# Products of 512 columns for the weight tiles outside U, with the bank's halves added by ScalarE and VectorE

## The chip, the cores and the metric

The kernel runs on one core of a Trainium2 chip. The metric is the device time of the program in microseconds (us), the median of several runs. Engines go by their names in the profile: PE is TensorE, DVE is VectorE, ACT is ScalarE, POOL is GpSimd, SP is SyncE, which issues the loads.

## The reference

256 tokens of width 1024 go through two blocks in float32. Cut to what matters here:

```python
def first_block(x, ...):
    z = rmsnorm(x, norm_gain) @ w_in
    a_in, a_gate, q, k, v, b_gp, g_logits = split(z)
    y_a = (multiscale_pool(a_in) * silu(a_gate)) @ w_proj_a
    y_b = (dilated_attention(q, k, v) * silu(b_gp)) @ w_proj_b
    gates = sigmoid(g_logits + b_gate)
    x = x + (gates[0] * y_a + gates[1] * y_b) @ w_out
    return rmsnorm(x, final_gain)

def second_block(x, ...):
    x = x + short_conv_mixer(rmsnorm(x))       # (gate_b * conv3(gate_c * h)) @ w_out
    x = x + peer(rmsnorm(x), layer 0)
    x = x + windowed_gqa(rmsnorm(x))           # q: 16 heads, k and v: 4 heads
    x = x + peer(rmsnorm(x), layer 1)
    return rmsnorm(x)

def peer(t):
    sc = (t @ w_q) against two sets of 128 subkeys, 8 heads
    idx, g = top 16 of the 16 x 16 best pairs, softmax
    h = t . u_tab[idx]
    return sum over idx of g * gelu(h) * v_tab[idx]
```

The kernel computes `peer` densely: all 16384 rows of `u_tab` meet all tokens (stage U), and `v_tab` likewise (stage V).

## The kernel before

The normed tokens stand transposed, 1024 channels as eight groups `k` of 128 partitions, with 256 tokens in a row. To keep float32 accuracy a value is held as two parts of the faster format `fp32r`: a high part, rounded, and a low part, the rest. Of two such numbers the kernel forms three products: high by high, high by low, low by high. The tokens' parts are `xh` and `xl`.

A weight tile is 128x1024: eight square pieces, one for each `k`, that give 128 outputs. `dense_t` (line 140) handles one: `fetch` has SP load it into `raw`; `split` (line 106) has ScalarE cast the high part `hi` (line 122) and VectorE, for some tiles POOL, subtract to get the low part `lo` (line 123); then `products` (line 133) makes 24 products of 256 columns (lines 136 to 138) that add up in the first half of a PSUM bank:

```python
        for i, ((ah, al), (bh, bl)) in enumerate(pairs):
            PE.matmul(out=ps, lhsT=ah, rhs=bh, start=first and i == 0, stop=False)
            PE.matmul(out=ps, lhsT=ah, rhs=bl, start=False, stop=False)
            PE.matmul(out=ps, lhsT=al, rhs=bh, start=False, stop=last and i == n - 1)
```

Weights come first in the product's names (`lhsT`), tokens second. `hi` and `lo` have three buffers each (`HL`), so the cast of tile t+3 waits for the last product of tile t. The banks of these tiles come from the pool `p_mm`, which has two; transposes (`p_tr`) have two, scores and accumulators (`p_acc`) four, which makes eight in all. The caller reads the bank and so sets it free.

The callers, in the program's order, and the number of tiles that the change touches:

- `qk` (line 622), 24 tiles of queries and keys of the first attention. The first six follow on each other; among the rest stand scores, transposes and values. Consumers are ScalarE's copies and, for group 0, `stacked` (line 149), two of ScalarE and two of VectorE.
- `rest` (line 508), 12 tiles: pooling input, `gate_a`, `gate_b`. The consumer is one ScalarE copy (lines 511 and 514); a silu follows for each gate (lines 523 and 524).
- `gate` (line 544), 16 tiles: a sigmoid on ScalarE (line 547). Four come first, then two before each `merge`, which has a weight tile of its own that is not changed.
- `streamed` in `conv_mixer` (line 722), 20 tiles in groups of three: gate `gb`, `gc` and `h`. ScalarE copies `gb` and `gc` (line 727); `h` stays in its bank until VectorE's `pr` (line 746) has multiplied it by `gc`. The sums of the short convolution (lines 750 and 752), `z` (line 756) and the parts `o` (lines 402 and 403) follow. ScalarE and VectorE also split a tile of the output weights for each group (`kept`).
- `query` of `peer` (line 955), 12 tiles in each of two layers: a ScalarE copy (line 957), then two products with the subkeys and VectorE's lists (from line 974).
- `query` of `gqa_mixer` (line 796), 8 tiles: `stacked` into `q_t` (lines 153 and 155), among scores (line 811), transposes and weighted sums.

Stage U (line 1171) calls `dense_t` for 256 tiles, and 360 tiles make up the 2880 products of each line. A scheduler orders the instructions of each engine at build time from the program's order; the split is issued with a priority 200 steps ahead (`AHEAD`), so that casts and subtractions come before work that stands earlier in the program. Each engine then runs its list strictly in that order, and waits where an instruction's input, or the room for its output, is not there.

Of the kernel before, what the change touches and what calls it, by code (L numbers as in the profile page):

```python
# [11 lines left out]
F32R = mybir.dt.float32r  # L12
# [3 lines left out]
AF = mybir.ActivationFunctionType  # L16
# [34 lines left out]
def two_blocks(ctx: ExitStack, tc: tile.TileContext, io, out):  # L51
# [26 lines left out]
    x = const.tile([P, 2, D], F32, name="x")  # L78
    sums = [const.tile([P, 4], F32, name=f"ss{a}") for a in range(2)]
    squares = const.tile([P, 512], F32, name="squares")  # L80
    xh = const.tile([P, 8, T], F32R, name="xh")
    xl = const.tile([P, 8, T], F32R, name="xl")
    iota_f = const.tile([P, P], BF16, name="iota_f")
    G.iota(iota_f, pattern=[[1, P]], base=0, channel_multiplier=0,
           allow_small_or_imprecise_dtypes=True)
# [20 lines left out]
    def split(raw, pool_share=0, into=None):  # L106
        with tc.high_priority(offset=AHEAD):
            return split_now(raw, pool_share, into)
# [31 lines left out]
    def dense_t(src, acts, pool_share=0):  # L140

        ah, al = acts
        hi, lo = split(fetch(src), pool_share)
        ps = bank(p_mm, "mm")[:, :T]
        products(ps, [((hi[:, k * P:(k + 1) * P], lo[:, k * P:(k + 1) * P]), (ah[:, k], al[:, k]))
                      for k in range(8)], True, True)
        return ps

    def stacked(ps, dst):

# [271 lines left out]
    def first_block(nxt):  # L422
        acts = xh, xl
        with ExitStack() as es:
# [81 lines left out]
                V.tensor_tensor(out=pooled[g], in0=pooled[g], in1=u[:, g, 8:8 + T], op=OP.subtract)  # L506

            def rest(n):
                ps = dense_t(io["w_rest"][n], acts)
                if n < 8:  # L510
                    S.copy(out=as_ordered(gate_a[:, n % 4] if n >= 4 else u[:, n, 8:8 + T]),
                           in_=ordered(ps))
                else:
                    S.copy(out=gate_b[:, n % 4], in_=ps)
                if 4 <= n < 8:
                    window(n - 4)
# [27 lines left out]
            def gate(n, i):  # L544
                c = 8 * i + n
                gt = w2.tile([P, T], F32, tag=f"gt{i}", name=f"gt{i}", bufs=3)
                S.activation(out=gt, in_=dense_t(io["w_rest"][12 + c], acts), func=AF.Sigmoid,
                             bias=b_gate[:, c:c + 1])
                gates[n, i] = gt

# [44 lines left out]
    def attention(acts, es1, at1, v_n, att, rest, loads):  # L595
# [25 lines left out]

        def qk(hp, g):
            n = g * 4 + hp
            ps = dense_t(io["w_qk"][n], acts, 2)
            if g:
                S.activation(out=q_t[hp][:, g - 1], in_=ps, func=AF.Copy, scale=0.125)
            else:
                stacked(ps, q_2[hp])
            ps = dense_t(io["w_qk"][12 + n], acts, 2)
            if g:  # L630
                S.copy(out=k_t[hp][:, g - 1], in_=ps)
                return
            for e, mine, _ in HALVES:
                S.copy(out=k_2[hp][mine, e], in_=ps[mine])
            for e, mine, _ in HALVES:
                V.tensor_tensor(out=k_l[hp][mine], in0=ps[mine], in1=k_2[hp][mine, e].bitcast(F32),  # L636
                                op=OP.subtract)
            for e, mine, other in HALVES:
                G.tensor_copy(out=k_2[hp][other, e], in_=k_2[hp][mine, e])
# [70 lines left out]
    def conv_mixer(entered, nxt):  # L710
        acts, nat = (xh, xl), entered.nat
        with ExitStack() as es:
# [7 lines left out]
            keep = keeper(cv, io["conv_w_out"])  # L720

            def streamed():
                return dense_t(io["conv_w_in"][next(tiles)], acts)

            def copied(tag):
                t = w2.tile([P, T], F32, tag=tag, name=tag)
# [37 lines left out]
    def gqa_mixer(entered, nxt):  # L764
        acts, nat = (xh, xl), entered.nat
        with ExitStack() as es:
# [27 lines left out]
            zl = b1.tile([P, 8, T], F32R, name="zl")  # L794

            def query(n):
                stacked(dense_t(io["attn_w_q"][n], acts, 3), q_t[:, 2 * n:2 * n + 2])

            def place(i):

# [127 lines left out]
    def peer(l, entered, nxt):  # L928
        acts, nat = (xh, xl), entered.nat
        with ExitStack() as es:  # L930
            with ExitStack() as es1:
# [19 lines left out]
                def query(n):  # L951
                    if n < 4:
                        q[n] = first[:, n]
                        return
                    ps = dense_t(io["peer_w_q"][l, n - 4], acts, 2)
                    q[n] = X[1][:, n].rearrange("p g t -> p (g t)")
                    S.copy(out=q[n], in_=ps)

# [419 lines left out]
```

## Time and profile before

| what | value |
|---|---|
| median of 3 runs | 2127.23 us (2122.63 to 2131.82) |
| profiled execution, its own time | 2128.48 us |
| its span | 2126.7 us |
| mean granted clock of PE | 0.992 of full speed |
| PE busy | 2089.0 us, 98% |
| PEld (weight loads, beside the products) busy | 1899.0 us, 89% |
| DVE, ACT, POOL busy | 1519.2, 1095.3, 216.4 us |
| DMA | 373.94 MB, mean 176 GB/s |

The page comes from the profiled execution. Its span runs from the first to the last recorded instruction. A busy time is a share of the whole; what a wait costs is read in the stage where it stands.

### The profile page before, as it was taken

To read this page: it belongs to the slowest core of one execution; us is meant where nothing else is said; L and a number is where in the kernel's file an instruction comes from. 1 tells how busy PE (TensorE), PEld (TensorE's weight loads), DVE (VectorE), ACT (ScalarE), POOL (GpSimd) and SP (SyncE) were. 2 spreads that over 40 slices of the span, in tenths; PEclk is the share of its full clock that TensorE was granted. 3 is DMA by queue.
4 is the path that set the end of the run, shared out by engine and by line. 5 is a ranking of instruction groups with operands and counts; after the bars stand their busy time and mean duration, and the time that the engine had idled before them with its cause. 6 is when DMAs were issued, how large, how long until landed. Compare 5 with 4: busy or idle time off the path is not lost. (4 is left out here: it accounts for less than half of the span.)

```text
span 2126.7 us, 37692 instructions
## 1 busy us (share of the span) xinstructions
PE 2089.0 (98%) x14288; PEld 1899.0 (89%) x14288; DVE 1519.2 (71%) x3101; ACT 1095.3 (52%) x1971; POOL 216.4 (10%) x119
## 2 busy tenths in 40 slices
PE   8999999999999999999999999999999999999998
PEld 7899989899999999888888777999999998888886
DVE  4456778699778887655656685998778885656565
ACT  4556645345555444555555574455554445555554
POOL 3220011162000000000000241540000000000000
PEclk9999999999999999999999999999999999999999
DMA  6645737255655555666666571566555556666664
GB/s 235 219 128 158 244 114 247 89 171 177 180 163 165 159 160 168 192 193 190 194 191 199 181 230 50 165 185 182 161 164 163 160 165 195 195 189 192 194 189 138
DMA packets 104437, 373.94 MB, mean 176 GB/s; under 512 B 12096, under 2 KB 14144, under 8 KB 103744
## 3 DMA queue, kind: packets, MB, share of 16 engines
q1 hardware_dynamic: 103968, 371.01, 56.1%
q8 instruction: 112, 1.84, 0.3%
q14 instruction: 69, 0.57, 0.1%
q10 hardware_dynamic: 288, 0.52, 0.1%
HBM read 370.44 MB, written 1.05 MB: 175 GB/s over the span
## 5 line engine op out<-in xcount | busy, mean ns | idle before, releaser
L123 DVE TENSOR_TENSOR lo<-raw,hi 128x1024 fp32r<-128x1024 f32 x532 | 650.6, 1223 | 260.2 <-ACT hi L122 256.9
L136 PE MATMUL mm<-xh,hi 128*128 128x256 f32 x2880 | 830.4, 288 | 0.4 <-DVE k_l L636 0.4
L138 PE MATMUL mm<-xh,lo 128*128 128x256 f32 x2880 | 814.3, 283 | 0.4 <-DVE lo L123 0.4
L137 PE MATMUL mm<-xl,hi 128*128 128x256 f32 x2880 | 814.1, 283 | 0.0
L122 ACT CAST hi<-raw 128x1024 fp32r<-128x1024 f32 x600 | 630.1, 1050 | 337.4 <-PE mm L137 192.9
L136 PEld LDWEIGHTS mm<-xh,hi 128*128 128x128 f32 x2880 | 551.5, 191 | 2.3 <-issue 1.3
L137 PEld LDWEIGHTS mm<-xl,hi 128*128 128x128 f32 x2880 | 551.8, 192 | 0.3
L138 PEld LDWEIGHTS mm<-xh,lo 128*128 128x128 f32 x2880 | 551.2, 191 | 0.8 <-DVE lo L123 0.8
L1204 PE MATMUL acc<-hi,al 128*128 128x512 f32 x976 | 304.1, 393 | 0.0
L1204 PE MATMUL acc<-lo,ah 128*128 128x512 f32 x976 | 302.4, 391 | 0.0
L1204 PE MATMUL acc<-hi,ah 128*128 128x512 f32 x976 | 301.5, 390 | 0.0
L1204 PEld LDWEIGHTS acc<-hi,ah 128*128 128x128 f32 x976 | 183.1, 188 | 41.8
L1204 PEld LDWEIGHTS acc<-hi,al 128*128 128x128 f32 x976 | 183.3, 188 | 39.7
L1204 PEld LDWEIGHTS acc<-lo,ah 128*128 128x128 f32 x976 | 183.3, 188 | 38.7
L1193 ACT CAST ah<-xa 128x256 fp32r<-128x256 f32 x200 | 81.2, 407 | 241.5 <-PE acc L1204 241.5
L123 POOL TENSOR_TENSOR lo<-raw,hi 128x1024 fp32r<-128x1024 f32 x70 | 171.6, 2452 | 267.5 <-ACT hi L122 256.0
L1194 DVE TENSOR_TENSOR al<-xa,ah 128x256 fp32r<-128x256 f32 x200 | 85.0, 426 | 99.0 <-PE acc L1204 99.0
L1109 DVE TENSOR_TENSOR o<-iota_k,ij 128x1024 f16<-128x1024 f16 x128 | 88.2, 689 | 48.5 <-PE G L1123 48.2
L298 POOL TENSOR_TENSOR enl<-raw,enh 128x1024 fp32r<-128x1024 f32 x5 | 12.4, 2478 | 867.3 <-ACT enh L297 867.3
L1133 ACT COPY xa<-G 128x240 f32<-128x240 f32 (+22 forms) x92 | 24.1, 262 | 148.2 <-DVE xa L1130 148.2
L1116 DVE TENSOR_TENSOR wi<-o,gt 128x512 f16<-128x512 f16 x256 | 96.5, 418 | 1.2
L1123 PE MATMUL G<-wi,o 128*128 128x128 f16 x1024 | 79.8, 220 | 0.0
(461 smaller groups left out, 2029.6 us busy)
## 6 DMA issues: line engine op xcount, KB each, us to landing
raw<-in_peer_u_dram SPq DMA_DIRECT2D x256, 512.0 KB, 3.6
raw<-in_peer_v_dram SPq DMA_DIRECT2D x256, 512.0 KB, 4.1
raw<-in_peer_w_q_dram SPq DMA_DIRECT2D x24, 512.0 KB, 3.7
raw<-in_conv_w_in_dram SPq DMA_DIRECT2D x20, 512.0 KB, 4.4
raw<-in_w_rest_dram SPq DMA_DIRECT2D x18, 512.0 KB, 3.7
raw<-in_w_qk_dram SPq DMA_DIRECT2D x16, 512.0 KB, 4.3
more<-in_w_rest_dram SPq DMA_DIRECT2D x10, 512.0 KB, 3.7
raw<-in_w_v_dram SPq DMA_DIRECT2D x8, 512.0 KB, 4.3
```

Source lines behind the costliest of these rows:

```text
L122: S.copy(out=hi, in_=raw)
L123: low = (G if on_pool else V).tensor_tensor(out=lo, in0=raw, in1=hi.bitcast(F32), op=OP.subtract)
L136: PE.matmul(out=ps, lhsT=ah, rhs=bh, start=first and i == 0, stop=False)
L137: PE.matmul(out=ps, lhsT=ah, rhs=bl, start=False, stop=False)
L138: PE.matmul(out=ps, lhsT=al, rhs=bh, start=False, stop=last and i == n - 1)
L1109: V.tensor_tensor(out=o.rearrange("p n (b c) -> p n b c", c=4), in0=iota_k.rearrange("p (b c) -> p b c", c=4).unsqueeze(1).to_broadcast(fo ...
L1116: V.tensor_tensor(out=wi[i].rearrange("p n (b c) -> p n b c", c=4), in0=o[:, 0:4].rearrange("p n (b c) -> p n b c", c=4), in1=gt[i][:, s]. ...
L1123: PE.matmul(out=ps[:, :, t], lhsT=o[:, 4 + t], rhs=wi[i][:, t], start=i == 0, stop=i == 1)
L1133: S.copy(out=dst[:, old:], in_=ps[:, i0 + old:i0 + n])
L1193: S.copy(out=act[0], in_=src)
L1194: V.tensor_tensor(out=act[1], in0=src, in1=act[0].bitcast(F32), op=OP.subtract)
L1204: PE.matmul(out=acc[a][half], lhsT=p[:, s], rhs=r[:, half * 512:(half + 1) * 512], start=i == 0 and w == 0, stop=i == P - 1 and w == 2)
```

## The change

The tokens' two parts become the halves of one tile `xx`, side by side for each `k`. A new function `dense_w` takes the place of `dense_t` in the six callers above; U keeps `dense_t`. For each `k` it makes one product of `hi` with 512 columns (`xh` and `xl`) into the whole bank, and one of `lo` with the 256 columns of `xh` into the first half: 16 products in place of 24. The second half of the bank then holds high by low. ScalarE copies it into one of the two halves of `squares`, and VectorE adds that to the first half, in the bank. Callers read the first half as before.

```diff
-    xh = const.tile([P, 8, T], F32R, name="xh")
-    xl = const.tile([P, 8, T], F32R, name="xl")
+    xx = const.tile([P, 8, 2, T], F32R, name="xx")
+    xh, xl = xx[:, :, 0], xx[:, :, 1]
...
+    def dense_w(src, pool_share=0):
+        hi, lo = split(fetch(src), pool_share)
+        ps = bank(p_mm, "mm")
+        for k in range(8):
+            s = slice(k * P, (k + 1) * P)
+            PE.matmul(out=ps, lhsT=hi[:, s], rhs=xx[:, k].rearrange("p w t -> p (w t)"),
+                      start=k == 0, stop=False)
+            PE.matmul(out=ps[:, :T], lhsT=lo[:, s], rhs=xh[:, k], start=False, stop=k == 7)
+        other = squares[:, count[0] % 2 * T:count[0] % 2 * T + T]
+        S.copy(out=other, in_=ps[:, T:])
+        V.tensor_tensor(out=ps[:, :T], in0=other, in1=ps[:, :T], op=OP.add)
+        return ps[:, :T]
...
-                ps = dense_t(io["w_rest"][n], acts)
+                ps = dense_w(io["w_rest"][n])
...
-                S.activation(out=gt, in_=dense_t(io["w_rest"][12 + c], acts), func=AF.Sigmoid,
+                S.activation(out=gt, in_=dense_w(io["w_rest"][12 + c]), func=AF.Sigmoid,
...
-            ps = dense_t(io["w_qk"][n], acts, 2)
+            ps = dense_w(io["w_qk"][n], 2)
...
-            ps = dense_t(io["w_qk"][12 + n], acts, 2)
+            ps = dense_w(io["w_qk"][12 + n], 2)
...
-                return dense_t(io["conv_w_in"][next(tiles)], acts)
+                return dense_w(io["conv_w_in"][next(tiles)])
...
-                stacked(dense_t(io["attn_w_q"][n], acts, 3), q_t[:, 2 * n:2 * n + 2])
+                stacked(dense_w(io["attn_w_q"][n], 3), q_t[:, 2 * n:2 * n + 2])
...
-                    ps = dense_t(io["peer_w_q"][l, n - 4], acts, 2)
+                    ps = dense_w(io["peer_w_q"][l, n - 4], 2)
```

The scheduler builds a new order from this. Three places show it. In these rows a name is a tile with its number, and the part behind the arrow is what is read; `mm` is a weight tile's bank. Numbers differ from one kernel to the other. The change's lines stand one lower in the helpers (123 for 122, 124 for 123), 16 lower in the callers (743 for 727, 762 for 746, 563 for 547); the new copy is line 161, the addition line 162.

ScalarE in the middle of the convolution, before:

```order
L122 CAST hi_3917<-raw_3915 128x1024
L727 COPY gb_3797<-mm_3804 128x256
L402 CAST o4h_3787<-z_3785 128x256
L122 CAST hi_3950<-raw_3948 128x1024
L727 COPY gc_3830<-mm_3837 128x256
L402 CAST kept4h_4027<-raw_4025 128x1024
L122 CAST hi_3982<-raw_3980 128x1024
L122 CAST hi_4034<-raw_4032 128x1024
```

The same place with the change (`mm_3326` is a gb tile, `mm_3353` the gc tile after it, `mm_3379` the h tile, which takes the bank of `mm_3326`; `hi_3448` takes the buffer of `mm_3353`'s high part):

```order
L123 CAST hi_3421<-raw_3419 128x1024
L161 COPY squares_81<-mm_3326 128x256
L418 CAST kept3h_3513<-raw_3511 128x1024
L123 CAST hi_3448<-raw_3446 128x1024
L418 CAST o3h_3309<-z_3307 128x256
L743 COPY gb_3319<-mm_3326 128x256
L161 COPY squares_81<-mm_3353 128x256
L743 COPY gc_3346<-mm_3353 128x256
L123 CAST hi_3474<-raw_3472 128x1024
L161 COPY squares_81<-mm_3379 128x256
L123 CAST hi_3520<-raw_3518 128x1024
```

Before, the copy of gb follows the cast that waits for the end of gb's own tile. With the change the copy of gb, two rows behind `hi_3448`, comes after a cast that waits for the end of the gc tile.

ScalarE at the first gate of the first block, before (`mm_2018` is the last `rest` tile, `mm_2058` the first gate):

```order
L122 CAST hi_2152<-raw_2150 128x1024
L514 COPY gate_b_282<-mm_2018 128x256
L524 ACTIVATE gate_b_282<-gate_b_282 128x1024
L122 CAST hi_2185<-more_2183 128x1024
L547 ACT_TABLE_LOAD
L547 ACTIVATE gt0_2051<-mm_2058,b_gate_286 128x256
```

With the change (`mm_1841` is the first gate; `hi_2009` takes the buffer of the second gate's high part):

```order
L123 CAST hi_1950<-more_1948 128x1024
L540 ACTIVATE gate_b_281<-gate_b_281 128x1024
L161 COPY squares_81<-mm_1841 128x256
L418 CAST yb0h_1900<-y_1898 128x256
L123 CAST hi_2009<-raw_2007 128x1024
L563 ACT_TABLE_LOAD
L563 ACTIVATE gt0_1834<-mm_1841,b_gate_285 128x256
```

The first gate's sigmoid followed one cast, and it now follows the second gate's cast, `hi_2009`, as well.

VectorE in the convolution, before:

```order
L123 TENSOR_TENSOR lo_3834<-raw_3831,hi_3833 128x1024
L403 TENSOR_TENSOR kept3l_3911<-raw_3908,kept3h_3910 128x1024
L746 TENSOR_TENSOR pr_3777<-mm_3752,gc_3713 128x4x4x16
L750 TENSOR_SCALAR y_3781<-pr_3777,taps_3338 128x256
L123 TENSOR_TENSOR lo_3866<-raw_3863,hi_3865 128x1024
```

With the change:

```order
L162 TENSOR_TENSOR mm_3353<-squares_81,mm_3353 128x256
L124 TENSOR_TENSOR lo_3475<-raw_3472,hi_3474 128x1024
L162 TENSOR_TENSOR mm_3379<-squares_81,mm_3379 128x256
L762 TENSOR_TENSOR pr_3398<-mm_3379,gc_3346 128x4x4x16
L766 TENSOR_SCALAR y_3402<-pr_3398,taps_3025 128x256
```

Between the low part of a later tile and the product `pr` there now stands the addition in the h tile's bank.

## Rows read from the trace of the kernel before

**Rows 1.** The page's part 1: engine, busy us (share of the span), instructions.

```profile
PE 2089.0 (98%) x14288; PEld 1899.0 (89%) x14288; DVE 1519.2 (71%) x3101; ACT 1095.3 (52%) x1971; POOL 216.4 (10%) x119
```

**Rows 2.** The page's part 5: group | busy, mean ns | idle before.

```profile
L136 PE MATMUL mm<-xh,hi 128*128 128x256 f32 x2880 | 830.4, 288 | 0.4 <-DVE k_l L636 0.4
```

**Rows 3.** Windows: us; busy of PE, PEld, DVE, ACT, POOL; PEclk, DMA, GB/s.

```profile
305.00:365.00 60.00, 60.00 (x488) 59.37 (x487) 50.85 (x78) 35.85 (x50) 2.41 (x1) 1.00 0.68 220
405.00:450.00 45.00, 44.92 (x380) 44.71 (x379) 41.75 (x240) 19.64 (x29) 21.59 (x9) 1.00 0.53 159
1240.00:1250.00 10.00, 6.96 (x32) 4.33 (x31) 8.38 (x16) 7.35 (x18) 6.33 (x4) 0.70 0.56 181
```

**Rows 4.** Timeline of ACT, convolution: start, us, what [idle before <-releaser].

```profile
329.66 1.05 ACT L122 CAST hi<-raw 128x1024 fp32r<-128x1024 f32 x1 [1.78 <-PE mm L137]
...
330.61 0.37 ACT L727 COPY gb<-mm 128x256 f32<-128x256 f32 x1
...
331.41 0.41 ACT L402 CAST o3h<-z 128x256 fp32r<-128x256 f32 x1 [0.44 <-DVE pr L745]
...
338.30 1.05 ACT L122 CAST hi<-raw 128x1024 fp32r<-128x1024 f32 x1 [1.78 <-PE mm L137]
```

**Rows 5.** Timeline of PE in the expert stage V.

```profile
1100.02 0.62 PE L1204 MATMUL acc<-lo,ah 128*128 128x512 f32 x2
...
1102.76 0.62 PE L1204 MATMUL acc<-lo,ah 128*128 128x512 f32 x2
```

**Rows 6.** Groups by line: two VectorE operations that read a bank.

```profile
L561 DVE TENSOR_TENSOR y<-pj,gt 128x256 f32<-128x256 f32 x16 | 6.5, 419 | 1.4 <-PE pj L138 1.4
...
L329 DVE TENSOR_TENSOR xl<-tr,xh 128x512 fp32r<-128x512 f32 x20 | 13.3, 688 | 18.0 <-ACT xh L328 17.9
```

**Rows 7.** Timeline of DVE in the convolution.

```profile
328.60 1.22 DVE L123 TENSOR_TENSOR lo<-raw,hi 128x1024 fp32r<-128x1024 f32 x1
...
329.74 1.00 DVE L752 SCALAR_TENSOR_TENSOR y<-pr,taps,y 128x256 f32<-128x256 f32 x2
...
336.36 0.60 DVE L746 TENSOR_TENSOR pr<-mm,gc 128x256 f32<-128x256 f32 x1
```

**Rows 8.** Waits of PE: line <- releaser: us in total, times, longest.

```profile
PE mm L136 <- DVE k_l L636: 0.4, 1, 0.4
...
PE acc L181 <- ACT o7h L402: 2.9, 1, 2.9
...
PE tr L413 <- DVE s L827: 4.9, 3, 3.0
```

**Rows 9.** Timeline of ACT from the last `rest` tiles to the first gate.

```profile
180.53 1.28 ACT L523 ACT_TABLE_LOAD   x1
...
181.82 1.06 ACT L523 ACTIVATE gate_a<-gate_a 128x1024 f32<-128x1024 f32 x1
...
196.47 1.28 ACT L547 ACT_TABLE_LOAD   x1
...
197.77 0.47 ACT L547 ACTIVATE gt<-mm,b_gate 128x256 f32<-128x256 f32 x1
```

**Rows 10.** Timeline of DVE, first expert query (MAX8 rows).

```profile
407.38 0.30 DVE L974 MAX8 xb<-sc 128x8 f32<-128x128 f32 x1 [10.07 <-PE sc L969]
...
422.89 0.30 DVE L974 MAX8 xb<-sc 128x8 f32<-128x128 f32 x1
```

**Rows 11.** Timeline of ACT in the first expert query.

```profile
409.09 1.05 ACT L122 CAST hi<-raw 128x1024 fp32r<-128x1024 f32 x1 [2.29 <-POOL lo L123]
...
422.37 1.05 ACT L122 CAST hi<-raw 128x1024 fp32r<-128x1024 f32 x1 [2.05 <-issue]
```

**Rows 12.** Timeline of ACT in window attention.

```profile
1226.17 1.05 ACT L122 CAST hi<-raw 128x1024 fp32r<-128x1024 f32 x1 [0.93 <-PE mm L137]
```

**Rows 13.** Timeline of DVE in window attention.

```profile
1227.92 0.87 DVE L155 SCALAR_TENSOR_TENSOR q_t<-mm,q_t 64x256 fp32r<-64x256 f32 x2 [0.91 <-ACT q_t L153]
```

**Rows 14.** Timeline of PE in window attention.

```profile
1237.73 0.60 PE L413 MATMUL tr<-ident,s 128*128 128x128 f32 x4
```

## The prediction

> **What bounds the kernel now.** I read the busy times first: TensorE is busy for 98% of the span, VectorE for 71%, ScalarE for 52% [rows 1]. Such a kernel ends earlier only where TensorE gets less to do, and later wherever TensorE is made to wait. Then the groups by line: the products of the weight tiles are 2880 on each of three lines, and the first of these lines has waited 0.4 us in all [rows 2]. So the 104 tiles that the change touches run without gaps now, and each new wait is paid in full. Then the stages: in a stretch of the convolution TensorE is busy for 60.00 of 60 us and VectorE for 50.85; in the expert query VectorE is busy for 41.75 of 45 [rows 3]. There VectorE has least to spare.
>
> **The products.** In the convolution every third tile has a cast that starts as the tile before ends, and these casts lie 8.64 us apart (329.66 and 338.30) [rows 4]: three tiles of 24 products, 0.1200 us each. Products of 512 columns stand in the expert stage V; the starts show twelve in 2.74 us, 0.2283 each [rows 5]. A tile costs 24 x 0.1200 = 2.880 us now, and 8 x (0.2283 + 0.1200) = 2.786 with the change: 0.094 less, and 9.7 us less for 104 tiles. That is the whole gain. The bounds: if the new pairs keep none of it, 0; if products cost their columns at 2.4 GHz and nothing else (6144 columns, 2.56 us), 0.32 per tile, 33 us. I take 9.7, since both intervals are rows.
>
> A rule of the Trainium skill speaks against this gain: "TensorE: Matmul & The Clock Gate", section "Back-to-back issue gap", gives an isolated product N/2.4 + 2.5 ns, so 109 and 216 ns here. By it a merged pair saves just 2.5 ns, an estimated 2 us for the 832 products that go, and the sum below would come out 8 us higher. The rows differ (120.0 and 228.3 ns, so a fixed part of some 13), and they decide. The section's sustained 131 ns for 512 columns is contradicted by the 228.3 likewise.
>
> **The added work.** Each tile gets a ScalarE copy of 128x256 (0.37 us, as at 330.61 [rows 4]) and a VectorE addition within the bank, which the trace does not show. The nearest rows are a product of bank and memory of the same size, 0.419, and a 128x512 subtraction that reads a bank, 0.688 [rows 6]. I take 0.42, as the size is the same; bounds 0.42 and 0.69. What costs is less the busy time than the place in the order.
>
> The pool has two banks. Before, tile t's bank is free after one consumer; now after copy, addition and consumer. The copy stands on ScalarE behind the cast of tile t+3's weights (1.05; the next starts 0.95 after it [rows 4]), since that cast takes the buffers that tile t held. The addition stands on VectorE behind the low part of those weights (1.22; the next starts 1.14 after it [rows 7]). And as the pieces of order show, ScalarE's consumers now stand behind the *next* tile's cast, which waits for the next tile's end: there the bank comes free after the tile that wanted it could have started. I walked each stage with these durations:
>
> (a) First six qk tiles, back to back: three waits, 0.36, 0.80 and 0.25, in place of the one of 0.4 [rows 8]: +1.0. The other 18 have scores and transposes between them: nothing. Without that cover they would be like the first six: +4.
>
> (b) Twelve `rest` tiles and the first two gates. The copies into the ordered halves give four small waits, 1.75 in all. Ahead of `rest(10)` `gate_b`'s copy stands behind a table load and a silu (1.28 and 1.06 [rows 9]): about 2. At the first gate the sigmoid follows a cast that waits for the *second* gate's end: 1.05, then a table load, 1.28, then 0.47, with the handovers between engines 2.95 in which the third gate has no bank. Before, table load and sigmoid end at 198.24, just in time [rows 9]. Sum +6.7. The other 14 gates have a merge tile of 2.88 between them, which covers this: nothing.
>
> (c) Convolution, 20 tiles in groups of three (gb, gc, h). The h tile wants gb's bank. The copy of gb stands behind a cast that waits for gc's end, 1.05, then an o cast, 0.41, and takes 0.37 itself: h starts 1.85 late. Two tiles on, a tile wants h's bank: cast 1.05, low part 1.14, addition 0.42 and `pr` 0.60 [rows 7] are 3.2 behind h's end, against 2.79 for the tile between: 0.45 late with the handovers. A group takes 3 x 2.786 + 2.30 = 10.66 us against 8.64 now. VectorE needs 50.85/60 x 8.64 = 7.32, and 3 x 0.42 more, 8.58, so the waits bound it. Five groups inside give 11.5, the other five tiles (two at the start, the last group) one long and two short waits, 2.75: +14.3. At the convolution's end, where TensorE waits 2.9 for the last o [rows 8], copy and addition come on top: +0.85.
>
> (d) Expert query, 12 tiles in each of two layers. VectorE works through lists: ten MAX8 (two a list) and two low parts lie in 15.51 us [rows 10], so 2.6 a list. Two tiles need two lists, one low part and two additions: 2 x 2.6 + 1.14 + 2 x 0.38 = 7.1 (0.42 less the overlap of neighbours). TensorE needs 6.46: its tile is 3.32 now (13.28 for four [rows 11]), 2.88 and 0.44 of scores. So 0.32 late per tile, 3.85 in a layer, of which the lists in hand cover 1.0. Twice 2.8: +5.6.
>
> (e) Window attention's query, 8 tiles. From a cast that starts at a tile's end to the end of `q_t` it is 2.62 now (1226.17 to 1228.79 [rows 12, 13]), and 3.5 with copy and addition. Three tiles with their scores take 11.6 (1226.17 to 1237.73 [rows 12, 14]), in the walk 14.7, and the products' 0.28 is in the 9.7 already: +3.4. The other five lie around the place where TensorE already waits 3.0 for `s` [rows 8]: +1.7. Sum +5.1.
>
> The waits: 1.0 + 6.7 + 14.3 + 0.85 + 5.6 + 5.1 = 33.5. Less 9.7: **+23.8**. U's 256 tiles keep their products. The orders of SP and POOL stay but for one load and two rows, and 68% of the DMA engines' time at most is used in the stages of [rows 3], so I price the queues at nothing. The profiled execution took 2128.48, 1.25 above the median of 2127.23. From the median the sum gives 2151; I say **2150**. Its own range, with the walks a third off, is 2139 to 2162.
>
> **The rivals.**
> *The cover holds.* My waits rest on which tile's end frees a cast's buffers. If the cast ahead of a consumer waits for one tile earlier, gb is copied while gc runs, and nothing is late. For it: ScalarE idles 1.78 before a cast [rows 4]. Against it: it spends these 1.78 waiting for just such an end, and the pieces of order. Then 9.7 less is all: 2117.5, not slower. It decides where the copy of gb ends before gc's tile does. Chance 0.14.
>
> *VectorE's busy time alone counts*, not ScalarE's order: 5.6 in the expert query, (8.58 - 8.36) x 7 = 1.5 in the convolution: 2124.6. Chance 0.09.
>
> *The fixed part goes.* The tiles take 2.56. That is 23.6 better, but the query stages, bound elsewhere, keep their 32 tiles' 7: 2134 with the waits, 2094 without any. Against it stand the 0.2283. Chance 0.07, half each.
>
> *The clock falls in the new gaps.* Where TensorE waits now, it fell: 0.70 granted on average from 1240 to 1250, with 6.96 of 10 us busy [rows 3], so partly the lower of its two levels. The convolution's 56 us of products at 0.85, halfway to full, take 10 more: 2160. Against it: the convolution's share, 8.4 of 10.7, stays higher than that row's. Chance 0.10. The Trainium skill says that cycling through banks with short idle times between groups makes the clock oscillate ("TensorE: Matmul & The Clock Gate", section "A second HAM failure mode: psum-queue depth-cycling"); no stretch read here cycles banks with such gaps, so the trace neither agrees nor differs.
>
> The order has 16 products per tile in place of 24: that the change would not do what it says is no rival.
>
> **How the numbers follow.** 0.5%, about 10.6 us, is what a measurement of this kernel can tell from no change. The forecast has 0.60. Slower: forecast, clock, and a little of the case at 2134: 0.72. Same: VectorE's case, the rest of 2134, most of the cover's: 0.23. Faster: 2094 and a little of 2117.5: 0.05. The range leaves out 2117.5 and 2094, 0.175 together: 2124 to 2164.
>
> **What would show it.** Pairs of 512 and 256 columns 0.348 us apart; new idle time of TensorE at the tiles' first product, released by ScalarE's copies of gb and `gate_b`, by the sigmoid and by `pr`; groups of 10.7 us in the convolution at a clock near 1.00; 2.8 us more in each expert query. I am wrong if the groups stay under 9 us, if the pair takes less than 0.33, or if the waits gather where I priced nothing, at the later qk tiles or gates.

## The result and the profile after

The change takes 2147.54 us (median of 6 runs, 2143.99 to 2148.54) against 2128.53 for the kernel before (6 runs): 1.0083 of its time, 95% interval 1.0071 to 1.0095. That is 19 us slower, and 2150 was forecast. The profiled execution has a span of 2142.2 us, 15.5 more than that of before. So the time lies near the forecast. But the sum behind the forecast was +23.8, the profiled execution shows +15.5, and the trace shows that the loss is spread in another way than the prediction had it.

First the page of the change: the busy times (where rows 1 stood), and the groups of the two new kinds of product.

```profile
PE 2090.4 (98%) x13456; PEld 1855.4 (87%) x13456; DVE 1554.1 (73%) x3205; ACT 1126.4 (53%) x2075; POOL 213.5 (10%) x119
...
L157 PE MATMUL mm<-xx,hi 128*128 128x512 f32 x832 | 301.9, 403 | 7.7 <-ACT gt L563 2.5
...
L159 PE MATMUL mm<-xx,lo 128*128 128x256 f32 x832 | 233.8, 281 | 0.0
```

TensorE is as busy as before in sum, 98%, though it makes 832 products fewer. The line of the first product has now waited 7.7 us, where it was 0.4 [rows 2]. The waits of TensorE (columns as in rows 8; line 197 is 181 of before, 429 is 413, 827 is 811) say for whom:

```profile
PE acc L197 <- ACT o7h L418: 4.3, 1, 4.3
...
PE tr L429 <- ACT hi L123: 2.7, 1, 2.7
...
PE tr L429 <- ACT q_t L169: 2.7, 1, 2.7
...
PE sc L827 <- DVE q_t L171: 2.5, 2, 1.9
...
PE mm L157 <- ACT gt L563: 2.5, 2, 1.7
...
PE mm L157 <- ACT gb L743: 1.6, 2, 0.8
...
PE mm L157 <- DVE q L171: 1.1, 3, 0.7
...
PE mm L157 <- ACT gate_b L530: 0.3, 1, 0.3
```

Of the four releasers that were forecast, the sigmoid `gt` and the copy `gb` are there; `gate_b` has 0.3, where about 2 was priced, and `pr` does not appear. And the waits at line 157 are only half of the 15.5 us. The rest does not stand there as idle time: other work was put into gaps, and the clock fell in two places. To see it I took the start of each tile's first product from both traces, and looked how the shift between them grows from stage to stage. The forecast's column is the prediction's own waits less 0.094 per tile.

| stretch, by the start of its first tile and of the next stretch's | forecast | measured |
|---|---|---|
| 24 qk tiles | -1.3 | -0.6 |
| 12 `rest` tiles and the first gates, to the first gate behind a merge tile | +5.4 | +6.5 |
| the other gates, and the rows up to the convolution | -1.3 | +0.2 |
| convolution and its output rows, to the first expert query | +13.3 | +7.6 |
| first expert query | +1.7 | -1.35 |
| U, V, and the norm behind them | 0 | -1.4 |
| window attention | +4.35 | +5.2 |
| second expert query | +1.7 | -1.3 |
| U, V and the end | 0 | +0.9 |
| sum | +23.8 | +15.8 |

(The first tile starts 0.33 us earlier in the change, so 15.8 is 15.5 in the span. One profile of each kernel lies behind a row. In the experiments below, stretches whose tiles are those of before still differ from this trace of before: by +1.6 to +2.2 in the convolution with its rows (numbers 4 to 6), and by 0.0, -3.0 and -3.0 in window attention (numbers 5, 6 and 12). In the two with -3.0 the clock stayed at 1.00 there; in the trace of before it is at 0.50 for 6.8 us, from 1244.1.)

**The convolution.** PE's timeline shows one group of three tiles there, from the gc tile at 341.87 to the next gc tile at 353.53:

```profile
341.87 0.47 PE L157 MATMUL mm<-xx,hi 128*128 128x512 f32 x1
...
344.72 0.40 PE L197 MATMUL acc<-kept2l,o2h 128*128 128x512 f32 x1
...
346.66 0.50 PE L197 MATMUL acc<-kept3h,o3h 128*128 128x512 f32 x1 [0.60 <-ACT o3h L418]
...
347.22 0.39 PE L157 MATMUL mm<-xx,hi 128*128 128x512 f32 x1
...
350.00 0.39 PE L157 MATMUL mm<-xx,hi 128*128 128x512 f32 x1
...
352.78 0.40 PE L197 MATMUL acc<-kept3h,o3l 128*128 128x512 f32 x1
...
353.53 0.47 PE L157 MATMUL mm<-xx,hi 128*128 128x512 f32 x1
```

The group takes 11.66 us, and 10.66 was forecast. But nine products of line 197, the output rows of the convolution (`o` by `kept`), lie in it (the first of each piece is shown). Nine times 0.2283 [rows 5] is 2.05, so the group itself takes 9.6. In the trace before, all these products came after the last tile, the first at 361.3. The scheduler has filled a part of the new gaps with them, and they are missing later: from the last tile of the convolution to the first of the expert query it is 33.86 us now, where it was 43.61. ScalarE's timeline shows the order that makes the gap:

```profile
344.30 1.05 ACT L418 CAST kept3h<-raw 128x1024 fp32r<-128x1024 f32 x1 [1.78 <-DMA raw<-in_conv_w_out_dram]
345.26 1.05 ACT L123 CAST hi<-raw 128x1024 fp32r<-128x1024 f32 x1
346.21 0.40 ACT L418 CAST o3h<-z 128x256 fp32r<-128x256 f32 x1
346.51 0.36 ACT L743 COPY gb<-mm 128x256 f32<-128x256 f32 x1
```

The gc tile ended at 344.7. The cast that takes its buffers came behind it, the o cast behind that, and only then was gb copied, done at 346.87: the h tile begins at 347.22, 2.5 us behind the end of gc. It is the order of ScalarE that was forecast (with 1.85), and 0.6 longer, because a cast of the output weights, which had waited for its load until 344.30, stands ahead of the other. TensorE's own wait in this gap, 0.60, is put down to the o cast, one place ahead of gb's copy.

**The first gate.** ScalarE, and the wait of TensorE that comes of it:

```profile
201.58 1.04 ACT L123 CAST hi<-raw 128x1024 fp32r<-128x1024 f32 x1
202.64 1.28 ACT L563 ACT_TABLE_LOAD   x1
203.94 0.47 ACT L563 ACTIVATE gt<-mm,b_gate 128x256 f32<-128x256 f32 x1
```

```profile
204.46 0.57 PE L157 MATMUL mm<-xx,hi 128*128 128x512 f32 x1 [1.75 <-ACT gt L563]
```

Cast, table load and sigmoid are the three of the forecast, and the third gate waits till the sigmoid has read the bank; 1.75 of it is seen as a wait, since products of the pooling branch were put in the gap.

**The clock and the expert query.** Windows of the change, columns as in rows 3: just behind that wait, the convolution, the expert query, and the last part of window attention.

```profile
204.70:208.20 3.50, 3.50 (x12) 2.94 (x12) 3.50 (x9) 2.50 (x6) 0.00 (x0) 0.51 0.45 150
309.00:385.00 76.00, 71.81 (x379) 58.61 (x377) 58.49 (x99) 42.02 (x70) 2.39 (x1) 1.00 0.58 181
420.00:448.00 28.00, 28.00 (x176) 24.91 (x175) 27.32 (x147) 13.78 (x27) 11.26 (x5) 1.00 0.56 170
1269.70:1280.00 10.30, 7.59 (x28) 5.85 (x30) 6.96 (x22) 5.23 (x14) 2.58 (x3) 0.50 0.52 193
```

For 3.5 us behind the first gate's wait the granted clock was the lower of the two levels, 0.51, and for 10.3 us in window attention 0.50 (0.70 over 10 us before [rows 3]). In the convolution it stayed at 1.00, although TensorE was busy for 71.81 of 76 us only. In the expert query TensorE has no gap at all. Its tiles start 3.22 us apart, 0.10 less than before [rows 11], to the last one:

```profile
425.56 0.47 PE L157 MATMUL mm<-xx,hi 128*128 128x512 f32 x1
...
428.78 0.47 PE L157 MATMUL mm<-xx,hi 128*128 128x512 f32 x1
...
432.00 0.47 PE L157 MATMUL mm<-xx,hi 128*128 128x512 f32 x1
```

And VectorE in the same place:

```profile
424.60 0.41 DVE L162 TENSOR_TENSOR mm<-squares,mm 128x256 f32<-128x256 f32 x1
...
424.92 0.08 DVE L991 MATCH_VALUE_LOAD xb<-xb,sc 128x8 f32 x1
...
425.45 0.29 DVE L990 MAX8 xb<-sc 128x8 f32<-128x128 f32 x1
...
426.63 0.29 DVE L990 MAX8 xb<-sc 128x8 f32<-128x128 f32 x1
```

The addition takes 0.41, the next starts 0.32 after it, and one half of a list (from one first MAX8 to the next) takes 1.18, so a list 2.36 where VectorE need not wait.

### The profile page after: what moved, and what is told of

It is laid out like the page before. It is cut to its first block, busy times and chain, and to the rows that moved or that the text cites. A ratio compares the mean times of both kernels' runs of the same rounds, so it can differ in the third digit from the quotient of the medians.

```text
span 2142.2 us, 36423 instructions
## 1 busy us (share of the span) xinstructions
PE 2090.4 (98%) x13456; PEld 1855.4 (87%) x13456; DVE 1554.1 (73%) x3205; ACT 1126.4 (53%) x2075; POOL 213.5 (10%) x119
## 3 DMA queue, kind: packets, MB, share of 16 engines
q8 instruction: 106, 1.74, 0.3%
## 4 chain that ended last, share of the span: by engine, by line
PE 88%; DVE 7%; ACT 2%; issue 1%; DMA 1%; SPq 0%; POOL 0%; ACTq 0%; DVEq 0%
PE acc L1220 32%; PE mm L137 11%; PE mm L139 10%; PE mm L138 10%; PE mm L157 8%; PE mm L159 4%; PE G L1139 3%; PE acc L197 2%; PE acc L875 1%; PE acc L137 1%; DVE lo L124 1%; PE acc L138 1%; PE acc L139 1%; ACT hi L123 1%; PE sc L985 1%
## 5 line engine op out<-in xcount | busy, mean ns | idle before, releaser
L137 PE MATMUL mm<-xx,hi 128*128 128x256 f32 x2048 | 590.6, 288 | 0.0
L139 PE MATMUL mm<-xx,lo 128*128 128x256 f32 x2048 | 578.9, 283 | 0.9 <-DVE lo L124 0.8
L138 PE MATMUL mm<-xx,hi 128*128 128x256 f32 x2048 | 578.5, 282 | 0.0
L139 PEld LDWEIGHTS mm<-xx,lo 128*128 128x128 f32 x2048 | 391.5, 191 | 1.7 <-DVE lo L124 1.7
L138 PEld LDWEIGHTS mm<-xx,hi 128*128 128x128 f32 x2048 | 391.9, 191 | 0.0
L137 PEld LDWEIGHTS mm<-xx,hi 128*128 128x128 f32 x2048 | 391.7, 191 | 0.2
L157 PE MATMUL mm<-xx,hi 128*128 128x512 f32 x832 | 301.9, 403 | 7.7 <-ACT gt L563 2.5
L159 PE MATMUL mm<-xx,lo 128*128 128x256 f32 x832 | 233.8, 281 | 0.0
L157 PEld LDWEIGHTS mm<-xx,hi 128*128 128x128 f32 x832 | 157.0, 189 | 49.7 <-issue 5.0
L159 PEld LDWEIGHTS mm<-xx,lo 128*128 128x128 f32 x832 | 157.8, 190 | 0.7
```

The costliest lines, as they stand in the source:

```text
L157: PE.matmul(out=ps, lhsT=hi[:, s], rhs=xx[:, k].rearrange("p w t -> p (w t)"), start=k == 0, stop=False)
L159: PE.matmul(out=ps[:, :T], lhsT=lo[:, s], rhs=xh[:, k], start=False, stop=k == 7)
```

## The experiments

The theory after this: the 16 products save what the rows priced, and what is lost comes from the places of copy, addition and consumer in the orders of ScalarE and VectorE, because two banks are all there is. The rivals: the engines' added busy time costs it, or the form of the product of 512 columns. Ratios are against the kernel before, with 95% intervals. That kernel's median was 2127.6 to 2130.1 beside numbers 1 to 12, so times of different numbers compare to some 2 us.

**1. Without copy and addition.**

```diff
-        other = squares[:, count[0] % 2 * T:count[0] % 2 * T + T]
-        S.copy(out=other, in_=ps[:, T:])
-        V.tensor_tensor(out=ps[:, :T], in0=other, in1=ps[:, :T], op=OP.add)
```

> The change without ScalarE's copy and VectorE's addition: the callers read the first half of the bank, so the product of the high weights with the tokens' low part is left out of the result, though it is computed. Theory (the 16 products save what the rows priced, and all that is lost is waits for the two banks behind copy and addition): 104 x 0.094 us come off the kernel before, about 2119 us, tiles of 2.79 us, and TensorE's new waits gone. Rival (the products of 512 columns save nothing here, the gaps only show it): about 2128.

2120.21 us, ratio 0.9959 (0.9945 to 0.9973). The group of the first product (columns as on the page):

```profile
L157 PE MATMUL mm<-xx,hi 128*128 128x512 f32 x832 | 299.8, 402 | 1.0 <-ACT gc L740 0.6 <-DVE k_l L649 0.4
```

The line waits 1.0 us, not 7.7. The products alone are worth 8.4 us, in line with the 9.7 forecast, and all that makes the change slower hangs on the two added operations. The rival of this run, that the products of 512 columns save nothing, falls.

**2. Three parts of 256 columns, copy and addition kept.**

```diff
-            PE.matmul(out=ps, lhsT=hi[:, s], rhs=xx[:, k].rearrange("p w t -> p (w t)"),
-                      start=k == 0, stop=False)
+            PE.matmul(out=ps[:, :T], lhsT=hi[:, s], rhs=xh[:, k], start=k == 0, stop=False)
             PE.matmul(out=ps[:, :T], lhsT=lo[:, s], rhs=xh[:, k], start=False, stop=k == 7)
+        for k in range(8):
+            PE.matmul(out=ps[:, T:], lhsT=hi[:, k * P:(k + 1) * P], rhs=xl[:, k],
+                      start=k == 0, stop=k == 7)
```

> The change with 24 products of 256 columns: high by low goes to the second half of the bank in eight products of its own at the end of the tile, and copy and addition stay. Theory (price of copy and addition is about 29 us in the profiled run, from 9.8 saved and 19 lost): 2147.5 + 9.8, about 2157 us. Rival (it is the form of the product of 512 columns, or its weight loads, that brings the gaps): back near the kernel before, under 2140.

2151.72 us, ratio 1.0112 (1.0093 to 1.0130). The loss is there without any product of 512 columns, so that rival falls too. Over the change it is 4 us by the medians, 6 by the ratios and 8.0 by the spans of the two profiled executions, and the two intervals leave room for the 9.8 that was expected. So how much of the shorter tile's saving is kept beside copy and addition, this run does not tell.

**3. Copy and addition with the split's priority.** The edit alters the order alone.

```diff
-        other = squares[...]
-        S.copy(...)
-        V.tensor_tensor(out=ps[:, :T], in0=other, in1=ps[:, :T], op=OP.add)
+        with tc.high_priority(offset=AHEAD):
+            other = squares[...]
+            S.copy(...)
+            V.tensor_tensor(out=ps[:, :T], in0=other, in1=ps[:, :T], op=OP.add)
```

> The change with copy and addition given the priority of the split (200 steps ahead), so that on ScalarE gb's copy in the convolution stands right behind them and ahead of the cast that waits for the next tile's end. Theory (the places in the order set the waits): the h tile's wait goes, the convolution's groups lose some 1.2 us each, 7 us in all, and the first gate's sigmoid no longer waits for the second gate's end, 2 us more: about 2139. Rival (the busy time that is added to ScalarE and VectorE sets them): 2147, no change.

2136.78 us, ratio 1.0041 (1.0028 to 1.0054): 10.8 less than the change, with the same work, so the rival of added busy time (2147) does not explain this part. In the convolution gb is now copied right behind the addition, with no cast in front:

```profile
353.13 1.05 ACT L123 CAST hi<-raw 128x1024 fp32r<-128x1024 f32 x1 [1.85 <-PE mm L157]
354.09 0.36 ACT L162 COPY squares<-mm 128x256 f32<-128x256 f32 x1
355.81 0.37 ACT L744 COPY gb<-mm 128x256 f32<-128x256 f32 x1 [1.36 <-DVE mm L163]
```

By the tiles' starts, `rest` and the first gates now cost 0.1 us where they cost 6.5, and window attention 1.9 for 5.2, while the convolution with its rows still costs 6.9. So the order is shown to set the loss at the gates. The time lies near the 2139 expected, but by another split; the forecast of 1.2 per group in the convolution did not come: TensorE now waits for gc's copy there (0.69, 0.44 and 0.41 us in three groups), so the gap has moved to another bank of the group.

**4. The convolution as before.** `streamed` returns `dense_t` again.

```diff
-                return dense_w(io["conv_w_in"][next(tiles)])
+                return dense_t(io["conv_w_in"][next(tiles)], acts)
```

> The change with the 24 products of before, and no copy and addition, in the convolution's 20 tiles alone. Theory from the two traces (the stretch from the first of these tiles to the first expert query grew by 7.6 us, since output rows now fill a part of the new gaps): 2147.5 - 7.6, about 2140. The prediction's own step for the convolution (14.3 + 0.85 of waits, less 1.9): about 2134. Rival (the convolution's waits are only moved from elsewhere): over 2145.

2138.95 us, ratio 1.0048 (1.0031 to 1.0064), 8.6 less than the change by the medians, 7.5 by the ratios and 5.4 by the tiles' starts (the stretch still shows +2.2). The convolution costs about what the two traces say, and not the 13.3 of the prediction.

**5 and 6. The expert queries alone, and with the other covered tiles.** Number 5 has `dense_w` in the two expert queries only, number 6 also in the gates from n = 2 on and in the qk tiles with `hp` over 0; all others call `dense_t`.

```diff
+            ps = dense_w(io["w_qk"][n], 2) if hp else dense_t(io["w_qk"][n], acts, 2)
...
+                S.activation(out=gt, in_=(dense_w(io["w_rest"][12 + c]) if n > 1 else
+                             dense_t(io["w_rest"][12 + c], acts)), func=AF.Sigmoid,
```

> The change in the two expert queries' 24 tiles alone. Theory (no wait there, each tile 0.10 shorter): 2.4 us less than the kernel before, about 2126. The prediction's own step (2.8 us of waits in each layer, less 1.1): about 2132, with tiles that lie further apart towards the end of the query.

> The change in 54 tiles alone, those where its trace shows no wait that is not made up for: the 24 of the two expert queries, the gates from the third merge tile on (12), and 18 of the qk tiles. Theory (VectorE still keeps up in the expert query, since a list takes 2.4 us there and not 2.6, and each tile saves 0.05 to 0.10): 24 x 0.10 + 12 x 0.05 + 18 x 0.09, 4.6 us less than the kernel before, about 2124, with tiles of the query 3.22 apart. The prediction's own step for the expert queries (5.6 us of waits): about 2130.

2126.36 us (0.9988, 0.9978 to 0.9997) and 2125.92 us (0.9988, 0.9978 to 0.9998). Both are a little faster than the kernel before, and the tiles of the queries lie 3.22 apart to the end. The prediction's step for the expert queries is wrong: they gain. What the 30 further tiles of number 6 add (some 2 us were expected) cannot be told from nothing here.

**7. Stage U too**, on top of number 3.

```diff
-                    ps = dense_t(io["peer_u"][l, i], acts, int(i < len(by_pool) and by_pool[i]))
+                    ps = dense_w(io["peer_u"][l, i], int(i < len(by_pool) and by_pool[i]))
```

> The version with copy and addition at the split's priority (2136.8), and dense_w in stage U's 256 tiles as well. Theory (a tile gains 0.09 where the engines keep up; VectorE is busy for 89.75 of 98 us early in U and 164.73 of 195 late, and gets 0.33 more per tile): late tiles gain, the first 35 or so of each layer lose as much as VectorE then lacks, 3 us: about 11 less, 2126. Rival one (every tile is covered, as in the expert query): 2113. Rival two (the wait for the two banks comes back in U, where the gelu on ScalarE sets them free behind a cast): 0.3 or more per tile, over 2200.

2239.16 us, ratio 1.0519 (1.0502 to 1.0536): rival two, 102 us more than number 3. The waits of TensorE in it:

```profile
PE mm L157 <- ACT xa L1196: 59.3, 74, 2.3
PE mm L157 <- ACT xb L1196: 17.4, 20, 1.2
```

77 of the 102 us are waits for the gelu (`xa`, `xb`), which frees the bank. My theory had only asked whether VectorE's time suffices. Late in U it has time left (164.41 of 195 us busy, where it is 164.73 in the change); TensorE waits for the two banks.

**8. The h tiles of the convolution as before**, on top of number 3: `dense_w` for gb and gc only.

```diff
-            def streamed():
-                return dense_w(io["conv_w_in"][next(tiles)])
+            def streamed(wide=False):
+                src = io["conv_w_in"][next(tiles)]
+                return dense_w(src) if wide else dense_t(src, acts)
...
-                S.copy(out=t, in_=streamed())
+                S.copy(out=t, in_=streamed(True))
```

> The version with copy and addition at the split's priority (2136.8), with the 24 products of before, and no copy and addition, for the h tiles of the convolution (6 of its 20, and the first). Theory (what is left of the convolution's waits is the h tile's bank, held over low part, addition and pr): the wait two tiles on goes, about 5 us: 2132. Rival (the waits that are left stand behind gb and gc, whose banks are still held longer): 2136 to 2138.

2135.17 us (2129.04 to 2138.67 in 10 runs), ratio 1.0029 (1.0017 to 1.0041). It overlaps number 3, so the medians leave it open. The tiles' starts put the convolution with its rows at +2.7 in place of +6.9. That is hardly more than the +2.2 of number 4, which has no new products there at all, and it speaks for the h bank.

**9 and 10. The sum in SBUF.** The addition writes over the copy, and the callers read it there; the bank is free after the addition. Number 10 has number 3's priority as well.

```diff
-        V.tensor_tensor(out=ps[:, :T], in0=other, in1=ps[:, :T], op=OP.add)
-        return ps[:, :T]
+        V.tensor_tensor(out=other, in0=other, in1=ps[:, :T], op=OP.add)
+        return other
```

> The change with one thing altered: the addition writes its sum over the copy in SBUF, not back into the bank, and the callers read it there. The bank is then free after copy and addition, and no consumer holds it. Theory (what is lost is that the consumers, behind the next tile's cast, still hold the bank): copy and addition end some 2.6 us behind a tile's end, inside the 2.79 of the next, so the waits of the convolution and of the first gate go, and most of the 9.8 appears: 2120 to 2126. Rival (the two halves of squares take the bank's place, since the copy of the tile after next waits for the consumer): 2136 or more, as with copy and addition early.

> The same, with copy and addition at the split's priority. Theory (consumers no longer hold the bank, so it matters little where they stand; copy and addition come a cast earlier in places): within 3 us of the one without, 2119 to 2125. Rival (the earlier copies push the consumers behind two more casts, and the halves of squares run out): 5 us or more slower than the one without.

2146.07 us (1.0088, 1.0075 to 1.0102) and 2131.35 us (1.0017, 1.0008 to 1.0027). Here the theory fell in the form I had given it. That consumers hold the bank is not what costs by itself: without the priority, the sum in SBUF gains nothing in all. TensorE's waits at the first product, number 9 and then number 10:

```profile
PE mm L157 <- DVE squares L162: 7.8, 9, 2.2
```

```profile
PE mm L157 <- DVE squares L163: 2.7, 5, 0.9
```

In number 9 the addition itself frees the bank too late, up to 2.2 us, because copy and addition still stand behind casts and low parts. With the priority these waits shrink to 2.7 us. The four versions together:

| | usual order | copy and addition first |
|---|---|---|
| sum in the bank | 2147.54 | 2136.78 |
| sum in SBUF | 2146.07 | 2131.35 |

Order is the first cause, and once it is mended the consumer's hold on the bank is worth another 5 us. By the tiles' starts the stages differ in this:

| stretch | change | 3: first | 9: SBUF | 10: both |
|---|---|---|---|---|
| `rest` and first gates | +6.5 | +0.1 | +3.3 | -1.7 |
| convolution with its rows | +7.6 | +6.9 | +7.3 | -2.0 |
| window attention | +5.2 | +1.9 | +8.3 | +3.8 |

At the gates each of the two helps by itself. In the convolution neither does, and both together take the whole loss away (number 12, with the same convolution, has +2.2, as untouched ones have). In window attention the sum in SBUF costs: TensorE waits 10.0 us for `q_t` before the scores there in number 9, and 2.5 in the change. Number 10 still lies 11 us above number 1. What makes this rest was not tried, and the added busy time is not ruled out for it.

**11. Stage U with the sum in SBUF and the priority.**

```diff
+                    ps = dense_w(io["peer_u"][l, i], int(i < len(by_pool) and by_pool[i]))
```

> The sum in SBUF, copy and addition at the split's priority, and dense_w in stage U's 256 tiles too. Theory (the waits that U had with dense_w, 0.43 us per tile, were for banks held by the gelu): they go, late tiles of U come 2.79 us apart, early ones are bound by VectorE (89.75 of 98 us busy before, 0.33 more per tile): some 10 less than without U, 2110. Rival (VectorE, at 84% late in U, has too little left with additions that stand behind low parts): 2130 or more.

2137.68 us, ratio 1.0050 (1.0035 to 1.0066). Freed of the gelu, the banks give back 101 of number 7's us, which shows that they were its cause. But U still does not gain over number 10: by the tiles' starts 8 us are lost in the first half of the first U and 3 won back in its second. So the time is the one that the rival gave (2130 or more), but the loss lies early in U and not late, where the rival had it. That VectorE is what is short early in U (89.75 of 98 us busy in the change) was not tried by itself.

**12. The best version found**: number 10, with `dense_t` in the window attention's query and in six of the qk tiles.

```diff
+                stacked(dense_t(io["attn_w_q"][n], acts, 3), q_t[:, 2 * n:2 * n + 2])
```

> The sum in SBUF, copy and addition at the split's priority, with the 24 products of before (no copy and addition) in the window attention's query and in six of the 24 qk tiles. Theory (in the version with all 104, window attention alone gives back 3.9 us and the other places hardly anything, so 90 tiles keep 0.05 to 0.10 each): 2131.4 - 4 to 6, about 2126, 2 to 3 us less than the kernel before. Rival (window attention loses as much for another reason, the work that moved into its gaps): 2130 or more.

2125.24 us, ratio 0.9984 (0.9972 to 0.9995), 3.4 us less than the kernel before by the ratio, and 22 less than the change. Of the versions that leave nothing out it is the fastest, by little: numbers 5 and 6 lie within its interval.

## Why the prediction was right, and where it was not

**Right.** The time (2150 against 2147.54), the sign, and the mechanism: a bank that comes free later because its readers stand behind other work. The pair of products takes 0.348 us in the convolution as priced; without the added operations the tiles gave 8.4 of the 9.7 us (number 1). Numbers 3 and 10 show that the places in the order and the hold on the bank, not the amount of work, make 11 and 16 of the 19 us; of the forecast releasers gb's copy and the sigmoid are there. The rule weighed against the rows (the Trainium skill, "TensorE: Matmul & The Clock Gate", section "Back-to-back issue gap") differs from the runs: by its 2.5 ns per merged pair number 1 would have gained an estimated 2 us, and it gained 8.4.

**The rivals.** The cover did not hold, and VectorE's time alone would have left 2124.6. The products kept their fixed part. The clock fell, but not where that rival put it: it stayed at 1.00 in the convolution, with its gaps (partly filled by then), and fell for 3.5 us at the first gate and 3.4 longer in window attention. At half the clock that is at most 3.4 us in the profiled execution, not 10. Over all six runs the mean granted clock is 0.9897, against 0.9923 in the ten runs of the kernel before beside numbers 1 to 4; an estimate from that, at half the clock, is 6 of the 19 us at most. The Trainium skill's remark on short idle times between groups ("TensorE: Matmul & The Clock Gate", section "A second HAM failure mode: psum-queue depth-cycling") is not borne out by the convolution's groups, which cycle through two banks with gaps at a clock of 1.00.

**Wrong, and luck.** The sum came out 8 us too high (+23.8 for +15.5 in the profiled execution), and 2150 lies near 2147.54 by luck: the median of the change lies 3.5 above its profiled execution, the median of the kernel before rose from 2127.23 to 2128.53 with three more runs, and 1 us was rounded off. Two terms were mis-sized by 5 to 6 us each, both too high:

- (c), the convolution: "A group takes 3 x 2.786 + 2.30 = 10.66 us against 8.64 now". The group takes 9.6 of its own, and nine output products were moved into its gaps, so the stretch with its rows lost 7.6 where 13.3 was forecast. Number 4 bears it out (8.6 by the medians, 5.4 by the tiles' starts). I had read the new orders of ScalarE and VectorE and not TensorE's, in which these products stand between the tiles. Output rows that used to stand at the end are cover for a gap.
- (d), the expert queries: "in 15.51 us, so 2.6 a list". That is the pace of a stretch in which TensorE had no gap, and not what a list needs. VectorE was busy for 15.09 of the 15.51 us, yet in nine places a step began some 0.3 us behind the one before it, or more, where 0.2 is usual, 1.2 us too much in sum. The trace of before shows both kinds:

```profile
414.05 0.28 DVE L976 MATCH_REPLACE8 rest<-xb,sc 128x128 f32<-128x128 f32 x1
414.24 0.29 DVE L974 MAX8 xb<-sc 128x8 f32<-128x128 f32 x1
414.45 0.28 DVE L978 MAX8 xb<-rest 128x8 f32<-128x128 f32 x1
...
415.23 0.28 DVE L976 MATCH_REPLACE8 rest<-xb,sc 128x128 f32<-128x128 f32 x1
415.55 0.30 DVE L978 MAX8 xb<-rest 128x8 f32<-128x128 f32 x1
```

  Where the first step of another half stands between, the next begins 0.19 later; where the reader of `rest` follows right behind its writer, 0.32. With the halves interleaved, as in most of the change, a list takes 2.36 and an addition 0.32 to the next start, so two tiles need 2 x 2.36 + 1.14 + 2 x 0.32 = 6.5 against 6.44: VectorE keeps up, but for what the banks in hand cover. The queries gained 1.3 each where 1.7 was to be lost.

Against these 11.8 us too many stand smaller ones too few: the `rest` tiles and first gates (+6.5 for 5.4, with at most 1.7 of it the clock), the later gates, which saved 0.05 per tile and lost 0.8 at the last one (+0.2 for -1.3), and window attention (+5.2 for 4.35, with at most 1.7 of the clock). The profiled execution, at 2143.99, is also the fastest of the change's runs, 3.5 below their median. The clock of each run goes with that: 0.991 in the two runs near 2144, 0.988 to 0.990 in the four above 2147. Where it fell in those four no trace shows.

## What to carry to other kernels

A cheaper product is worth what it saves only while the result leaves its bank as fast as before: count what now stands between the end of a tile and the free bank, and where each of it stands in its engine's list. If a step must be added there, give it the priority of the work that it would otherwise queue behind, and let it write to SBUF; in all, order came first here, and in the convolution only both together helped. And do not take an engine's cost from the pitch of a stretch that another engine paces: a busy share of 15.09 in 15.51 us did not tell the two apart, and the rows in which its steps follow closest did.

## What was not expected of the hardware

The pair of a 512-column and a 256-column product does not have one interval. Between the merge tiles the first starts of two pairs lie 0.36 apart, in the convolution 0.35:

```profile
226.15 0.40 PE L157 MATMUL mm<-xx,hi 128*128 128x512 f32 x1
...
226.51 0.40 PE L157 MATMUL mm<-xx,hi 128*128 128x512 f32 x1
```

```profile
335.57 0.39 PE L157 MATMUL mm<-xx,hi 128*128 128x512 f32 x1
...
335.92 0.40 PE L157 MATMUL mm<-xx,hi 128*128 128x512 f32 x1
```

Over a tile that makes the saving 0.05 us there and 0.10 here (2.82 and 2.78 to the next tile, where both had some 2.88). What differs between the two places was not tried.

The clock at the first gate follows the wait there. In the four profiles in which TensorE waits 1.74 to 2.17 us at one stroke between 202.7 and 206.9 us (the change and numbers 2, 4 and 9), the granted clock falls to 0.50 or 0.51 within 1 us of its end; in the ten others, which have no such wait there, it is 1.00 from 196 to 214 us.
